# Weight-block additions of a seven-product MLP moved from VectorE to accumulating DMAs of GpSimd's queue

## The chip, the cores and the metric

The kernel runs on one core of a Trainium2 chip. The metric is the device time of one execution in microseconds. The engines are TensorE (PE: matmul; PEld: its weight load), VectorE (DVE), ScalarE (ACT), GpSimd (POOL) and SyncE (SP), which here only issues DMAs. Each engine works through its own instructions in order, and waits on semaphores for the others.

## The reference, cut to what matters

Two layers over 1024 tokens of width 1024. Each has a mixer (a gated MLP with a delta rule in layer 0, differential attention in layer 1), an MLP, and a gate at its end. The change is in the MLP:

```python
for layer in range(DEPTH):                       # 2
    ...
    hn = rms_norm(h, ln_mlp[layer])
    h = h + jnp.square(jax.nn.relu(hn @ w_mlp1[layer])) @ w_mlp2[layer]    # 1024 x 4096, 4096 x 1024
    gate = jax.nn.sigmoid(rms_norm(h, ln_ple[layer]) @ w_ple_gate[layer])
    h = h + (p[layer] @ w_ple_proj[layer]) * gate
```

## The kernel before

**Precision.** Every fp32 operand is split into hi (a rounded copy, ScalarE, line 224) and lo (operand minus hi, VectorE, line 225). A product is three matmuls, hi·hi, hi·lo and lo·hi (`mm3`, all recorded at line 78). In the profile a raw weight block is `raw` or `keep`, its hi and lo are `w`; the raw activations are `graw`, their hi and lo `g`.

**Seven products instead of eight.** Both matrix products of the MLP are taken as 2×2 blocks by the Strassen–Winograd scheme: sums and differences of weight blocks (a11, a12, a21, a22) and of activation blocks, seven products, and additions of the results. The helper `tt` (line 283) is one VectorE tensor_tensor and records nearly all those additions.

**First product (`front`, `rest`).** The 4096 hidden features go in 8 chunks `c`. `front(c)` makes two of the seven products, `rest(c)` five. A weight block is two tiles of 128×2×256 (256 KB each), loaded by `block` through SP (line 331). Before, `rest` loads a21, a22 and a11 and forms on VectorE s1 = a21 + a22 (into slot "B", of which there is one), a11 − a21 and s1 − a11; later it loads a12 and subtracts the last of these from it. The results, after relu and square, and their sums are saved to DRAM as `gd`, seven sets (`save`, line 354).

**Second product (`product2(n)`).** The seven products run in the order n = 1, 6, 5, 3, 7, 4, 2. Each has 16 steps `kt`; a step takes one weight block of 128×512 from `left(n, kt)` and one activation block of `gd`, splits both, and issues 4 × 3 matmuls of 512 columns, 192 per product. The blocks a11 (n = 1) and s1 (n = 6) stay in tiles `keep`, which lie in the space of the half's hi and lo tiles. Before, n = 6 loads a21 into `keep` and a22 into `raw`, adds them in `keep`, and subtracts a11 into `raw`; n = 5 uses `keep` as it is; n = 3 loads a12, adds a11 and subtracts s1; n = 7 loads a21 and subtracts; n = 4 and 2 only load. Results are added into `acc` and `u` after a product, on VectorE. `fetch` loads the residual `acc` in between.

**What sets the order.** A scheduler places the instructions of each engine from the program order and the pools. Pools: 8 `raw` tiles (`RB`), 12 `w` tiles (6 steps), 4 `graw` slots, 4 pairs of `g`. Every DMA of `load` (line 323) is further held behind the last matmul of the step `AHEAD` = 7 steps earlier. SP issues in order: a `graw` load that waits for its slot holds back every weight load behind it.

**At the end of a layer** `take_hs(0)` forms the row scales of the first half and broadcasts them (`rows`: 8 matmul records of `aux<-ident,r` and a copy by ScalarE, line 273).

Of the kernel before, what the change touches and what calls it, by code (L numbers as in the profile page):

```python
# [116 lines left out]
class Trunk:  # L117
# [158 lines left out]
    def mlp(self, x, x_tags, gain, w1, w2, gain_next, h_dram, p, last):  # L276
# [5 lines left out]
        def tt(out, a, b, op):  # L282
            nc.vector.tensor_tensor(out, a, b, op)  # L283
            return out
# [37 lines left out]

            self.pe.behind(nc.sync.dma_start(out, src), marks[-AHEAD])

        def block(c, r, k):

            out = []
            for i in range(2):
                out.append(self.raw(2, 256))
                r0, c0 = (4 * k + 2 * i) * P, c * 512 + r * 256  # L330
                nc.sync.dma_start(out[i], w1[r0 : r0 + 2 * P, c0 : c0 + 256].rearrange("(k p) m -> p k m", p=P))
            return out

        def product(raws, b, ps=None):

# [38 lines left out]
        def rest(c):  # L374
            u, g11 = us.pop(c), g11s.pop(c)
            g12, g21, g22 = (tiles((f"c{8 + 2 * i}", f"c{9 + 2 * i}"), "g") for i in range(3))
            v, g2 = ([self.sp.tile([P, HT], F32, tag=f"{n}{h}", name=self.nm("v"), bufs=1) for n in ("sqs", "rb")] for h in range(2))
            s1 = self.slot("B", [P, 2, 2, 256], F32, "s1")
            s1 = [s1[:, i] for i in range(2)]
            a21, a22, a11 = block(c, 1, 0), block(c, 1, 1), block(c, 0, 0)  # L380
            for i in range(2):
                tt(s1[i], a21[i], a22[i], ALU.add)
                tt(a21[i], a11[i], a21[i], ALU.subtract)
                tt(a11[i], s1[i], a11[i], ALU.subtract)
            ps = product(a21, t3)
            for i in range(2):
                nc.scalar.copy(v[i], ps[i])
            ps6 = product(a11, t2)
            if not t4:
                t4.extend(make_t4())  # L390
            for i in range(2):
                tt(u[i], u[i], ps6[i], ALU.add)
                tt(v[i], u[i], v[i], ALU.add)
            product(a22, t4, ps)
            for i in range(2):
                tt(g21[i], u[i], ps[i], ALU.add)
                relu2(g21[i], g21[i])
                tt(g11[i], g21[i], g11[i], ALU.subtract)
            save(3, c, g21)
            save(7, c, g11)  # L400
            if not t1:
                t1.extend(make_t1())
            ps = product(s1, t1)
            for i in range(2):
                tt(g22[i], v[i], ps[i], ALU.add)
                relu2(g22[i], g22[i])
            save(2, c, g22)
            a12 = block(c, 0, 1)
            for i in range(2):
                tt(a12[i], a12[i], a11[i], ALU.subtract)  # L410
            product(a12, b22, ps)
            for i in range(2):
                tt(g12[i], u[i], ps[i], ALU.add)
                relu2(g12[i], g12[i])
            save(1, c, g12)
            for i in range(2):
                tt(g2[i], g11[i], g12[i], ALU.add)
            save(6, c, g2)
            for i in range(2):
                tt(g22[i], g22[i], g2[i], ALU.subtract)  # L420
                tt(g21[i], g21[i], g2[i], ALU.subtract)
            save(4, c, g22)
            save(5, c, g21)
# [49 lines left out]
        def kept(half, k):  # L473

            return self.hp.tile([P, 1, HT], F32, tag=f"{('hi', 'lo')[k % 2]}{half}{k // 2}", name=self.nm("keep"))

        def load2(t, r, k, kt):

            r0 = (kt // 2) * 512 + k * 256 + (kt % 2) * P
            load(t, w2[r0 : r0 + P, r * 512 : (r + 1) * 512].rearrange("(k p) m -> p k m", p=P))  # L480
            return t

        def left(n, kt):
            def raw():
                return self.raw(1, HT)

            if n == 1:
                keep[0, kt] = load2(kept(1, kt), 0, 0, kt)
                return keep[0, kt]
            if n == 6:  # L490
                s1 = keep[1, kt] = load2(kept(0, kt), 1, 0, kt)
                s2 = load2(raw(), 1, 1, kt)
                tt(s1, s1, s2, ALU.add)
                return tt(s2, s1, keep[0, kt], ALU.subtract)
            if n == 5:
                return keep[1, kt]
            if n == 3:
                s4 = load2(raw(), 0, 1, kt)
                tt(s4, s4, keep[0, kt], ALU.add)
                return tt(s4, s4, keep[1, kt], ALU.subtract)  # L500
            if n == 7:
                s3 = load2(raw(), 1, 0, kt)
                return tt(s3, keep[0, kt], s3, ALU.subtract)
            return load2(raw(), int(n == 4), 1, kt)
# [42 lines left out]
            tt(acc[q][1], acc[q][1], ps[q], ALU.add)  # L547
        ps = product2(6)
        for q in range(4):
            tt(u[q], u[q], ps[q], ALU.add)  # L550
        ps = product2(5, beside={4: (0, 4), 8: (0, 0), 12: (1, 4)})
        for q in range(4):
            tt(acc[4 + q][0], acc[4 + q][0], ps[q], ALU.add)
# [12 lines left out]
        for q in range(4):  # L566
            tt(acc[4 + q][1], acc[4 + q][1], ps[q], ALU.add)
            put(4 + q, 1)
        self.take_hs(0)
        ps = product2(2)  # L570
        for q in range(4):
            tt(acc[q][1], acc[q][1], ps[q], ALU.add)
# [1604 lines left out]
```

## Time and profile before

| | us |
|---|---|
| three timed runs | 2472.01, 2472.32, 2473.27 (median 2472.32) |
| the profiled execution | 2478.68 |
| its span | 2477.0 |
| TensorE without work in the span | 18.3 |
| first product of layer 0's MLP | about 490 to 776 |
| second product of layer 0, n = 1, 6, 5, 3, 7 | from 776, 820, 865, 909 and 953 on |
| second product of layer 1, n = 1, 6, 5, 3, 7 | from 2045, 2089, 2134, 2178 and 2224 on |

Times are microseconds from the span's start. A stretch of the profile lists for each engine the busy time and in brackets the instructions, then the mean TensorE clock (1.00 is full), the share of time in which the core's 16 DMA engines were busy, and the rate they moved. In a timeline, brackets at a row's end hold the idle time before it and what ended it. In the chain of work that ended last, each piece is followed back to what released it.

### The profile page before, as it was taken

The page shows a single profiled execution, that of the slowest core. Times are in us where ns is not written, and L with a number is a line of the kernel's source. Part 1 is how long each engine was busy: PE and PEld are TensorE (multiplying, and loading weights), DVE is VectorE, ACT ScalarE, POOL GpSimd, SP SyncE. Part 2 cuts the span into 40 slices and gives each one's busy share as a digit, 9 for nine tenths or more (in the row PEclk, how much of TensorE's full clock was granted, in tenths as well). Part 3 has the DMA queues.
Part 4 walks back from the last instruction along what each step waited for, and adds up shares of the span by engine and source line. Part 5 has one row for each costly group of instructions (what it writes and reads, how often), then busy time and mean ns, then how long its engine had stood idle before and what let it go on. Part 6 is the DMA issues. An engine that isn't in the chain of part 4 may idle for free.

```text
span 2477.0 us, 39903 instructions
## 1 busy us (share of the span) xinstructions
PE 2458.7 (99%) x13501; PEld 2104.9 (85%) x13501; DVE 1857.3 (75%) x3622; ACT 1315.9 (53%) x2701; POOL 320.2 (13%) x304
## 2 busy tenths in 40 slices
PE   9999999999999999999999999999999999999999
PEld 7898998888888888888899999988878888878887
DVE  7787766697667879566568888876886677788677
ACT  6554474465455435454366666664745455435543
POOL 0231231000000000000244443341000000000010
PEclk9999999999999999999999999999999999999999
DMA  7385655467557755553347776787375558657772
GB/s 245 113 261 119 173 172 164 140 179 245 162 175 249 255 181 194 185 176 113 115 107 165 162 175 154 195 230 236 130 236 190 174 181 286 218 178 221 224 247 91
DMA packets 555029, 459.08 MB, mean 185 GB/s; under 512 B 248260, under 2 KB 416456, under 8 KB 554824
## 3 DMA queue, kind: packets, MB, share of 16 engines
q1 hardware_dynamic: 524472, 451.28, 59.8%
q10 hardware_dynamic: 29584, 3.68, 1.0%
q8 instruction: 106, 1.74, 0.3%
q0 software_dynamic: 768, 1.57, 0.2%
q14 instruction: 99, 0.81, 0.1%
HBM read 322.04 MB, written 134.37 MB: 184 GB/s over the span
## 4 chain that ended last, share of the span: by engine, by line
PE 91%; DMA 4%; DVE 3%; ACT 1%; issue 1%; SPq 0%; POOL 0%; DVEq 0%; ACTq 0%
PE mm L78 80%; PE po L78 3%; PE aux L78 2%; PE qk L78 2%; DMA raw<-in_w_mlp_dram 1%; PE tr L81 1%; DMA spill<-early 0%; DMA early<-g_dram 0%; DVE raw L283 0%; DMA aT<-a_dram 0%; DMA a_dram<-lg 0%; PE pkq L78 0%; PE pks L78 0%; PE aux L81 0%; DVE w L225 0%
## 5 line engine op out<-in xcount | busy, mean ns | idle before, releaser
L78 PE MATMUL mm<-g,w 128*128 128x512 f32 x2592 | 603.1, 394 | 2.3 <-DVE acc L283 1.8
L224 ACT CAST w<-raw 128x512 fp32r<-128x512 f32 x598 | 364.4, 617 | 446.9 <-PE mm L78 381.5
L78 PEld LDWEIGHTS mm<-g,w 128*128 128x128 f32 x2592 | 487.7, 188 | 115.5 <-ACT g L224 2.2
L78 PE MATMUL mm<-hi,w 128*128 128x512 f32 x1728 | 552.9, 397 | 0.0
L78 PE MATMUL mm<-w,hi 128*128 128x256 f32 (+2 forms) x2528 | 500.4, 294 | 0.5 <-DVE w L225 0.4
L225 DVE TENSOR_TENSOR w<-raw,w 128x512 fp32r<-128x512 f32 (+1 forms) x510 | 347.6, 690 | 163.9 <-ACT w L224 152.9
L78 PEld LDWEIGHTS mm<-w,hi 128*128 128x128 f32 x2528 | 400.2, 188 | 14.5 <-DVE w L225 0.6
L78 PEld LDWEIGHTS mm<-hi,w 128*128 128x128 f32 x1728 | 324.9, 189 | 73.7
L78 PE MATMUL mm<-w,lo 128*128 128x256 f32 (+2 forms) x1264 | 367.7, 292 | 0.0
L78 PE MATMUL mm<-lo,w 128*128 128x512 f32 x864 | 340.7, 395 | 0.0
L78 PE MATMUL mm<-t,w 128*128 128x512 f32 x1152 | 270.7, 394 | 0.9 <-ACT w L224 0.7
L78 PEld LDWEIGHTS mm<-t,w 128*128 128x128 f32 x1152 | 216.3, 188 | 52.2 <-ACT w L224 1.2
L78 PEld LDWEIGHTS mm<-w,lo 128*128 128x128 f32 x1264 | 237.8, 188 | 5.4
L78 PEld LDWEIGHTS mm<-lo,w 128*128 128x128 f32 x864 | 162.9, 188 | 36.7
L224 ACT CAST g<-graw 128x512 fp32r<-128x512 f32 x216 | 132.6, 617 | 36.7 <-PE mm L78 15.8
L225 DVE TENSOR_TENSOR g<-graw,g 128x512 fp32r<-128x512 f32 x216 | 146.9, 684 | 5.6 <-DMA gd<-g 3.8
L1067 ACT ACTIVATE lg<-lg,nm 128x128 f32<-128x128 f32 (+7 forms) x128 | 99.2, 775 | 75.0 <-DVE nm L1064 73.2
L265 POOL TENSOR_TENSOR r<-ms,mhalf 128x4 f32<-128x4 f32 x12 | 12.5, 1043 | 948.1 <-DVE ms L263 920.9
L225 POOL TENSOR_TENSOR w<-raw,w 128x512 fp32r<-128x512 f32 (+1 forms) x88 | 113.9, 1316 | 132.2 <-ACT w L224 100.5
L349 ACT ACTIVATE g<-g 128x512 f32<-128x512 f32 x96 | 60.3, 631 | 111.1 <-DVE g L283 107.2
L1064 DVE CUSTOM_DVE_ANT_0 lg<-qk,al 128x512 f32<-128x512 f32 (+3 forms) x128 | 72.3, 568 | 25.8 <-PE qk L78 22.1
L78 PE MATMUL mm<-ohi,w 128*128 128x512 f32 x256 | 86.0, 400 | 0.2 <-DVE aT L1281 0.2
(344 smaller groups left out, 3554.1 us busy)
## 6 DMA issues: line engine op xcount, KB each, us to landing
raw<-in_w_mlp_dram SPq DMA_DIRECT2D x352, 256.0 KB, 3.2
graw<-gd SPq DMA_DIRECT2D x224, 256.0 KB, 2.7
gd<-g SPq DMA_DIRECT2D x192, 256.0 KB, 3.1
raw<-in_w_ple_gate_dram SPq DMA_DIRECT2D x76, 256.0 KB, 3.5
acc<-h_dram SPq DMA_DIRECT2D x64, 256.0 KB, 4.4
keep<-in_w_mlp_dram SPq DMA_DIRECT2D x64, 256.0 KB, 4.5
raw<-in_w_in_e_dram SPq DMA_DIRECT2D x60, 256.0 KB, 3.7
h_dram<-acc SPq DMA_DIRECT2D x48, 256.0 KB, 2.3
```

Source lines behind the costliest of these rows:

```text
L78: self._next(self.engine.matmul(*a, **k))
L81: self._next(self.engine.transpose(*a, **k))
L224: self.nc.scalar.copy(hi, src)
L225: (lo_engine or self.nc.vector).tensor_tensor(lo, src, f32(hi), ALU.subtract)
L265: nc.gpsimd.tensor_tensor(r, ms, self.mhalf[:, 0:4], ALU.pow)
L349: nc.scalar.activation(g, src, AF.Relu)
L1064: nc.vector.tensor_tensor_reduce(out=lg[:, k0:k1], in0=ps[:, : k1 - k0], in1=al[:, u0 + k0 : u0 + k1], scale=-1.0, scalar=3.0e38 if c == 0 ...
L1067: nc.scalar.activation(lg[:, :n], lg[:, :n], AF.Exp, bias=nm[:, r, nch - 1 : nch], scale=-1.0, accum_out=me.sums[:, b, r : r + 1])
```

## The change

In the first product a11 is loaded before a22; the differences are a11 − a21 and from that minus a22, so the product `ps6` has the other sign and is subtracted from u. s1 is no longer added on VectorE: SP loads a21 into slot "B", and GpSimd's queue adds a22 to it in the DMA (`accum_op=ALU.add`). a12 is added in the same way onto the tile of a11, behind that tile's split, instead of an own load and a subtraction.

In the second product n = 6 loads a21 into `keep` and lets GpSimd's queue add a22; VectorE then takes a11 minus that, in place (one operation rather than two, the sign turned). n = 5 loads a21 again, into `raw`, and adds a22 by DMA. n = 3 adds a12 by DMA onto `keep`, without a load and without VectorE. n = 7, 4 and 2 are as they were. The last layer's `take_hs(0)` leaves out the broadcast of the row scales, which nothing reads there.

```diff
--- before.py
+++ after.py
@@ -322,14 +322,21 @@
 
             self.pe.behind(nc.sync.dma_start(out, src), marks[-AHEAD])
 
-        def block(c, r, k):
-
-            out = []
+        def source(c, r, k, i):
+            r0, c0 = (4 * k + 2 * i) * P, c * 512 + r * 256
+            return w1[r0 : r0 + 2 * P, c0 : c0 + 256].rearrange("(k p) m -> p k m", p=P)
+
+        def block(c, r, k, out=None):
+
+            out = out or [self.raw(2, 256) for _ in range(2)]
             for i in range(2):
-                out.append(self.raw(2, 256))
-                r0, c0 = (4 * k + 2 * i) * P, c * 512 + r * 256
-                nc.sync.dma_start(out[i], w1[r0 : r0 + 2 * P, c0 : c0 + 256].rearrange("(k p) m -> p k m", p=P))
+                nc.sync.dma_start(out[i], source(c, r, k, i))
             return out
+
+        def add_block(c, r, k, out):
+
+            for i in range(2):
+                nc.gpsimd.dma_start(out[i], source(c, r, k, i), accum_op=ALU.add)
 
         def product(raws, b, ps=None):
 
@@ -377,19 +384,21 @@
             v, g2 = ([self.sp.tile([P, HT], F32, tag=f"{n}{h}", name=self.nm("v"), bufs=1) for n in ("sqs", "rb")] for h in range(2))
             s1 = self.slot("B", [P, 2, 2, 256], F32, "s1")
             s1 = [s1[:, i] for i in range(2)]
-            a21, a22, a11 = block(c, 1, 0), block(c, 1, 1), block(c, 0, 0)
+            a21, a11, a22 = block(c, 1, 0), block(c, 0, 0), block(c, 1, 1)
             for i in range(2):
-                tt(s1[i], a21[i], a22[i], ALU.add)
                 tt(a21[i], a11[i], a21[i], ALU.subtract)
-                tt(a11[i], s1[i], a11[i], ALU.subtract)
+                tt(a11[i], a21[i], a22[i], ALU.subtract)
+            block(c, 1, 0, s1)
+            add_block(c, 1, 1, s1)
             ps = product(a21, t3)
             for i in range(2):
                 nc.scalar.copy(v[i], ps[i])
             ps6 = product(a11, t2)
+            add_block(c, 0, 1, a11)
             if not t4:
                 t4.extend(make_t4())
             for i in range(2):
-                tt(u[i], u[i], ps6[i], ALU.add)
+                tt(u[i], u[i], ps6[i], ALU.subtract)
                 tt(v[i], u[i], v[i], ALU.add)
             product(a22, t4, ps)
             for i in range(2):
@@ -405,10 +414,7 @@
                 tt(g22[i], v[i], ps[i], ALU.add)
                 relu2(g22[i], g22[i])
             save(2, c, g22)
-            a12 = block(c, 0, 1)
-            for i in range(2):
-                tt(a12[i], a12[i], a11[i], ALU.subtract)
-            product(a12, b22, ps)
+            product(a11, b22, ps)
             for i in range(2):
                 tt(g12[i], u[i], ps[i], ALU.add)
                 relu2(g12[i], g12[i])
@@ -474,10 +480,18 @@
 
             return self.hp.tile([P, 1, HT], F32, tag=f"{('hi', 'lo')[k % 2]}{half}{k // 2}", name=self.nm("keep"))
 
+        def source2(r, k, kt):
+            r0 = (kt // 2) * 512 + k * 256 + (kt % 2) * P
+            return w2[r0 : r0 + P, r * 512 : (r + 1) * 512].rearrange("(k p) m -> p k m", p=P)
+
         def load2(t, r, k, kt):
 
-            r0 = (kt // 2) * 512 + k * 256 + (kt % 2) * P
-            load(t, w2[r0 : r0 + P, r * 512 : (r + 1) * 512].rearrange("(k p) m -> p k m", p=P))
+            load(t, source2(r, k, kt))
+            return t
+
+        def add2(t, r, k, kt):
+
+            self.pe.behind(nc.gpsimd.dma_start(t, source2(r, k, kt), accum_op=ALU.add), marks[-AHEAD])
             return t
 
         def left(n, kt):
@@ -488,16 +502,12 @@
                 keep[0, kt] = load2(kept(1, kt), 0, 0, kt)
                 return keep[0, kt]
             if n == 6:
-                s1 = keep[1, kt] = load2(kept(0, kt), 1, 0, kt)
-                s2 = load2(raw(), 1, 1, kt)
-                tt(s1, s1, s2, ALU.add)
-                return tt(s2, s1, keep[0, kt], ALU.subtract)
+                s2 = keep[1, kt] = add2(load2(kept(0, kt), 1, 0, kt), 1, 1, kt)
+                return tt(s2, keep[0, kt], s2, ALU.subtract)
             if n == 5:
-                return keep[1, kt]
+                return add2(load2(raw(), 1, 0, kt), 1, 1, kt)
             if n == 3:
-                s4 = load2(raw(), 0, 1, kt)
-                tt(s4, s4, keep[0, kt], ALU.add)
-                return tt(s4, s4, keep[1, kt], ALU.subtract)
+                return add2(keep[1, kt], 0, 1, kt)
             if n == 7:
                 s3 = load2(raw(), 1, 0, kt)
                 return tt(s3, keep[0, kt], s3, ALU.subtract)
@@ -547,7 +557,7 @@
             tt(acc[q][1], acc[q][1], ps[q], ALU.add)
         ps = product2(6)
         for q in range(4):
-            tt(u[q], u[q], ps[q], ALU.add)
+            tt(u[q], u[q], ps[q], ALU.subtract)
         ps = product2(5, beside={4: (0, 4), 8: (0, 0), 12: (1, 4)})
         for q in range(4):
             tt(acc[4 + q][0], acc[4 + q][0], ps[q], ALU.add)
@@ -566,7 +576,7 @@
         for q in range(4):
             tt(acc[4 + q][1], acc[4 + q][1], ps[q], ALU.add)
             put(4 + q, 1)
-        self.take_hs(0)
+        self.take_hs(0, rows=not last)
         ps = product2(2)
         for q in range(4):
             tt(acc[q][1], acc[q][1], ps[q], ALU.add)
```

By count: VectorE makes 160 tensor_tensor operations fewer, GpSimd's queue issues 160 accumulating DMAs of 256 KB, and the second product moves 144 weight blocks per layer instead of 112.

How it moves the instructions, in layer 0. First VectorE in the middle of n = 6; before, step 12 is the tile keep_1731, its second block raw_1732, its w numbers 1733 and 1734, and the g of steps 9 and 10 are g_1716 and g_1723:

```order
L283 TENSOR_TENSOR keep_1731_9332<-keep_1731_9332,raw_1732_9334 128x512
L225 TENSOR_TENSOR w_1720_9283<-raw_1718_9278,w_1719_9282 128x512
L283 TENSOR_TENSOR raw_1725_9306<-keep_1724_9304,keep_1613_8864 128x512
L283 TENSOR_TENSOR raw_1732_9334<-keep_1731_9332,keep_1619_8888 128x512
L225 TENSOR_TENSOR g_1716_9261<-graw_1714_9258,g_1715_9260 128x512
L283 TENSOR_TENSOR keep_1738_9360<-keep_1738_9360,raw_1739_9362 128x512
L225 TENSOR_TENSOR w_1727_9311<-raw_1725_9306,w_1726_9310 128x512
L283 TENSOR_TENSOR raw_1739_9362<-keep_1738_9360,keep_1625_8912 128x512
L225 TENSOR_TENSOR w_1734_9339<-raw_1732_9334,w_1733_9338 128x512
L225 TENSOR_TENSOR g_1723_9289<-graw_1721_9286,g_1722_9288 128x512
```

After, steps 11 to 13 are keep_1697, keep_1703 and keep_1709, and the g of steps 8 to 10 are g_1684, g_1690 and g_1696:

```order
L283 TENSOR_TENSOR keep_1697_9266<-keep_1597_8848,keep_1697_9266 128x512
L225 TENSOR_TENSOR w_1693_9245<-keep_1691_9240,w_1692_9244 128x512
L225 TENSOR_TENSOR g_1684_9199<-graw_1682_9196,g_1683_9198 128x512
L225 TENSOR_TENSOR w_1699_9271<-keep_1697_9266,w_1698_9270 128x512
L225 TENSOR_TENSOR g_1690_9225<-graw_1688_9222,g_1689_9224 128x512
L283 TENSOR_TENSOR keep_1703_9292<-keep_1603_8872,keep_1703_9292 128x512
L283 TENSOR_TENSOR keep_1709_9318<-keep_1609_8896,keep_1709_9318 128x512
L225 TENSOR_TENSOR w_1705_9297<-keep_1703_9292,w_1704_9296 128x512
L225 TENSOR_TENSOR g_1696_9251<-graw_1694_9248,g_1695_9250 128x512
```

Of the two operations on each block, the sum into `keep` is gone; the subtraction now stands on `keep` itself, with the subtractions of steps 12 and 13 ahead of the g of step 10.

Then SP in the same place, before (graw_1721 is step 10's, graw_1728 step 11's):

```order
L323 DMA raw_1725_9306<-in_w_mlp2_dram 128x512
L323 DMA graw_1721_9286<-gd_966_5752 128x512
L323 DMA keep_1731_9332<-in_w_mlp2_dram 128x512
L323 DMA raw_1732_9334<-in_w_mlp2_dram 128x512
L323 DMA graw_1728_9314<-gd_966_5752 128x512
L323 DMA keep_1738_9360<-in_w_mlp2_dram 128x512
L323 DMA raw_1739_9362<-in_w_mlp2_dram 128x512
```

And after (graw_1694 is step 10's, keep_1703 step 12's):

```order
L323 DMA graw_1688_9222<-gd_965_5751 128x512
L323 DMA keep_1697_9266<-in_w_mlp2_dram 128x512
L323 DMA graw_1694_9248<-gd_966_5752 128x512
L323 DMA keep_1703_9292<-in_w_mlp2_dram 128x512
L323 DMA graw_1700_9274<-gd_966_5752 128x512
L323 DMA keep_1709_9318<-in_w_mlp2_dram 128x512
```

One weight load of two per step is gone from SP; a step's weight load stands behind the activation load of two steps before. The second block now goes through GpSimd's queue, where the accumulates of the steps follow each other.

Last VectorE at the start of n = 3, where the results of n = 5 are added up, before (raw_1879 to raw_1903 are a12 blocks, acc and u results):

```order
L225 TENSOR_TENSOR w_1875_9967<-raw_1873_9962,w_1874_9966 128x512
L225 TENSOR_TENSOR g_1866_9921<-graw_1864_9918,g_1865_9920 128x512
L283 TENSOR_TENSOR acc_1533_8582<-acc_1533_8582,u_1540_8589 128x512
L283 TENSOR_TENSOR acc_1533_8582<-acc_1533_8582,u_1541_8590 128x512
L283 TENSOR_TENSOR acc_1533_8582<-acc_1533_8582,u_1542_8591 128x512
L283 TENSOR_TENSOR raw_1885_10014<-raw_1885_10014,keep_1589_8764 128x512
L283 TENSOR_TENSOR raw_1891_10040<-raw_1891_10040,keep_1595_8792 128x512
L993 MEMSET ql_2524_12565 128x512
L283 TENSOR_TENSOR raw_1897_10066<-raw_1897_10066,keep_1601_8816 128x512
L283 TENSOR_TENSOR raw_1885_10014<-raw_1885_10014,keep_1696_9192 128x512
L283 TENSOR_TENSOR raw_1891_10040<-raw_1891_10040,keep_1703_9220 128x512
L225 TENSOR_TENSOR w_1881_9993<-raw_1879_9988,w_1880_9992 128x512
```

And after, a few steps into n = 3:

```order
L225 TENSOR_TENSOR w_1868_10018<-keep_1679_9188,w_1867_10017 128x512
L225 TENSOR_TENSOR w_1873_10041<-keep_1685_9214,w_1872_10040 128x512
L225 TENSOR_TENSOR g_1866_10001<-graw_1864_9998,g_1865_10000 128x512
L225 TENSOR_TENSOR w_1878_10064<-keep_1691_9240,w_1877_10063 128x512
L225 TENSOR_TENSOR g_1871_10024<-graw_1869_10021,g_1870_10023 128x512
L225 TENSOR_TENSOR w_1883_10087<-keep_1697_9266,w_1882_10086 128x512
L225 TENSOR_TENSOR g_1876_10047<-graw_1874_10044,g_1875_10046 128x512
L225 TENSOR_TENSOR w_1888_10110<-keep_1703_9292,w_1887_10109 128x512
```

The two additions on every a12 block are gone; a step has one w and one g split.

## The prediction

> **What bounds the kernel now.** First the page: the busy row, then the chain of work that ended last.
>
> ```profile
> span 2477.0 us, 39903 instructions
> PE 2458.7 (99%) x13501; PEld 2104.9 (85%) x13501; DVE 1857.3 (75%) x3622; ACT 1315.9 (53%) x2701; POOL 320.2 (13%) x304
> PE 91%; DMA 4%; DVE 3%; ACT 1%; issue 1%; SPq 0%; POOL 0%; DVEq 0%; ACTq 0%
> ```
>
> TensorE is busy for 2458.7 of 2477.0 us. Whatever the change does on VectorE, it can win only what TensorE idles (18.3 us over the whole kernel) or loses to a lower clock. So the second view is busy time by stretch, one stretch per MLP stage, to see how much of that lies where additions are removed. The rows are the second half of layer 0's first MLP product (633 to 776), its MLP2 products 1, 6, 5, 3 (776 to 953), the opening of layer 1's first MLP product, and layer 1's product 3.
>
> ```profile
> core 0: us, PE busy (x) PEld busy (x) DVE busy (x) ACT busy (x) POOL busy (x), PEclk, DMA share, GB/s
> 633.00:776.00 143.00, 143.00 (x619) 116.06 (x618) 98.12 (x156) 73.35 (x129) 0.00 (x0) 1.00 0.55 184
> 776.00:820.00 44.00, 44.00 (x192) 35.73 (x191) 30.57 (x50) 23.16 (x42) 0.00 (x0) 1.00 0.86 291
> 820.00:865.00 45.00, 45.00 (x197) 36.55 (x196) 38.77 (x65) 21.32 (x38) 0.00 (x0) 1.00 0.77 248
> 865.00:909.00 44.00, 44.00 (x192) 35.81 (x191) 31.71 (x51) 17.92 (x32) 0.00 (x0) 1.00 0.60 190
> 909.00:953.00 44.00, 43.43 (x188) 34.73 (x187) 42.34 (x70) 18.41 (x32) 3.03 (x2) 1.00 0.58 190
> 1756.00:1812.00 56.00, 54.56 (x241) 43.44 (x240) 51.07 (x85) 36.69 (x66) 1.01 (x1) 1.00 0.40 118
> 2178.00:2224.00 46.00, 44.22 (x185) 35.49 (x184) 40.42 (x68) 17.76 (x32) 0.00 (x0) 0.96 0.55 174
> ```
>
> The reader is to see that the MLPs already run without a gap except at three places: product 3 of layer 0 (0.57 us idle), product 3 of layer 1 (1.78 us idle, and a mean clock of 0.96 over 46 us, another 1.84 us), and the opening in layer 1 (1.44 us). VectorE's 38.8 busy of 45 us in product 6 cost TensorE nothing. The largest gap is explained by the chain that ended last in layer 1's product 3, and by the queue's timeline a little earlier.
>
> ```profile
> 2172.61 0.42 SPq L323 DMA_DIRECT2D raw<-in_w_mlp_dram  x1
> ...
> 2175.53 0.69 DVE L283 TENSOR_TENSOR raw<-raw,keep 128x512 f32<-128x512 f32 x1 [0.55 <-DMA raw<-in_w_mlp_dram]
> ...
> 2177.34 0.68 DVE L225 TENSOR_TENSOR g<-graw,g 128x512 fp32r<-128x512 f32 x1
> ...
> 2178.05 0.32 SPq L323 DMA_DIRECT2D graw<-gd  x1
> ...
> 2178.42 0.43 SPq L323 DMA_DIRECT2D raw<-in_w_mlp_dram  x1
> ```
>
> ```profile
> 2178.42 2.89 DMA raw<-in_w_mlp_dram
> ...
> 2183.23 0.61 DVE g L225
> ...
> 2184.22 4.79 DMA raw<-in_w_mlp_dram
> ...
> 2190.25 0.69 DVE acc L283
> 2190.94 0.14 issue
> 2191.08 9.15 PE mm L78 x32
> ```
>
> This is a closed loop: a weight block lands, VectorE's addition takes it, a g split further back in the same in-order engine follows, that frees a graw slot, SP issues the graw load and only then the next weight load. One turn is 2178.42 − 2172.61 = 5.81 us for two steps; four products in 953 − 776 = 177 us make a step 2.77 us, so TensorE needs 5.54 for two. The loop loses a little per turn, and when one load takes 4.79 us instead of 2.89 the lead is gone: TensorE stands, then runs at a lower clock.
>
> **The change part by part.** What leaves VectorE, by form of instruction:
>
> ```profile
> L283 DVE TENSOR_TENSOR raw<-raw,raw 128x512 f32<-128x512 f32 x64 | 43.7, 686 | 27.6 <-DMA raw<-in_w_mlp_dram 27.4
> L283 DVE TENSOR_TENSOR raw<-raw,keep 128x512 f32<-128x512 f32 x64 | 43.1, 691 | 8.4 <-DMA raw<-in_w_mlp_dram 8.1
> L283 DVE TENSOR_TENSOR keep<-keep,raw 128x512 f32<-128x512 f32 x32 | 22.0, 688 | 12.1 <-DMA raw<-in_w_mlp_dram 12.0
> L283 DVE TENSOR_TENSOR s<-raw,raw 128x512 f32<-128x512 f32 x32 | 21.5, 688 | 8.6 <-DMA raw<-in_w_mlp_dram 8.5
> ```
>
> All 64 raw<-raw,keep (product 3), all 32 keep<-keep,raw (product 6), all 32 s<-raw,raw, and 32 of the 64 raw<-raw,raw (the a12 part) go: 64 × 0.691 + 64 × 0.688 + 32 × 0.686 = 110.2 us of VectorE. Nearly all of it lies beside a TensorE without a gap and is worth nothing in itself. What it is worth:
>
> *Product 3.* Per step, two of four VectorE operations and SP's weight load go; the accumulate needs no earlier load and waits behind no graw. The loop above no longer exists: 0.57 + 1.78 + 1.84 = **4.2 us**. Next late there would be the g path alone, two operations (1.4 us) per 2.77 us step.
>
> *Opening of layer 1.* There VectorE is the chain:
>
> ```profile
> 1800.32 1.20 DVE u L283 x2
> 1801.52 0.60 DVE w L225
> 1802.12 0.67 DVE s L283 x2
> ...
> 1808.07 1.28 DVE g L283 x2
> ...
> 1811.61 3.50 PE mm L78 x14
> ```
>
> The s pair (two times 0.6) leaves it, so **1.2** of the 1.44 us. In layer 0's opening nothing idles.
>
> *Last layer's unused row broadcast:*
>
> ```profile
> 2333.66 1.06 PE L78 MATMUL aux<-ident,r 128*128 128x128 f32 x8
> ...
> 2334.47 1.86 PE L78 MATMUL mm<-g,w 128*128 128x512 f32 x7
> ```
>
> The next matmul starts 0.81 us after the first of the eight: **0.8 us**. Signs and the order of subtractions cost nothing: as many operations of the same form.
>
> The ceiling is 4.2 + 1.2 + 0.8 = **6.2 us**, 0.25%.
>
> What is added: 32 accumulates per layer in the first product, 48 in the second, and in product 5 a reload of 16 blocks that were kept before. In the first product 16 MB of loads stay as many; DMA is busy 0.55 and POOL 0.00 there, so I cost it at nothing; that cover is the whole front of the next chunk between the request of s1 and its use. If it is gone, product s1 of a chunk waits. The first s1 of each layer is requested before the stage ahead has ended, and its accumulate waits in POOL's order for its load. Behind it stand, in layer 0, the last chunk's factor fo and its product with z; in layer 1 three lo splits of the output weights and the last block's of. POOL's rows there:
>
> ```profile
> 417.89 1.01 POOL L1915 TENSOR_TENSOR fo<-so,mhalf 128x4 f32<-128x4 f32 x1 [13.69 <-DVE so L1913]
> ...
> 1716.09 1.37 POOL L1128 TENSOR_TENSOR of<-osq,mhalf 128x4 f32<-128x4 f32 x1 [25.15 <-DVE osq L1126]
> ```
>
> POOL idles 13.7 and 25.2 us ahead of these, so a load of 3 to 4 us fits in: nothing; without that cover, up to 4 us per layer.
>
> *Product 6, the one added wait.* VectorE's subtraction now waits for load, then accumulate. Behind it in VectorE's order stands an older g split, which frees graw, behind which SP holds the next load. In the new order (its rows stand with the change) a turn advances three or four steps, 3.5 × 2.77 = 9.7 us. The turn costs 0.3 (graw issue) + load + accumulate + 2 to 3 VectorE operations at 0.6 (1.5). The loads of product 6, and the nearest rows for a DMA of POOL's queue against SP's:
>
> ```profile
> graw<-gd SPq DMA_DIRECT2D x17, 256.0 KB, 2.9
> keep<-in_w_mlp_dram SPq DMA_DIRECT2D x12, 256.0 KB, 4.0
> ```
>
> ```profile
> by_token<-t SPq DMA_DIRECT2D x48, 64.0 KB, 2.6
> by_token<-t POOLq DMA_DIRECT2D x16, 64.0 KB, 4.5
> ```
>
> Load: 2.9 to 4.0. Accumulate: no row shows one. Lower bound 2.9 (as an SP load), upper bound 9 (twice 4.5, if the second operand is read in a second pass). I take 4.5, the nearest row, since it has the queue. The turn is then 0.3 + 2.9 + 4.5 + 1.5 = 9.2, or 10.3 with the slower load: even with the 9.7 that TensorE needs. Over five turns of a product the slower one loses 3 us, inside the two to three steps by which operands run ahead (5.5 to 8 us: there are four g pairs, one of them in use). So I take 0. At 9 us it would be (0.3 + 4 + 9 + 1.5 − 9.7) × 5 = 25, less a lead of 7: 18 us per layer, the upper end. In product 5 nothing of VectorE waits between load and split, and loads run further ahead; the same prices, so also 0.
>
> The Trainium skill bears on this price: "DMA: Bandwidth & Descriptors", section "Anatomy of one DMA — SWDGE (gpsimd) path", fits 2.0 us plus bytes / 436e3 for one DMA of that path, so 2.6 us for 256 KB, and the turn would be 7.3. The trace speaks against it: 4.5 us for 64 KB, where the fit gives 2.15.
>
> *DMA engines.* Product 1 moves 291 GB/s at a share of 0.86, so 338 at full share: 0.775 us of all engines per 256 KB. With loads seven steps ahead, product 6's stretch holds 9 × 3 of its own, 7 × 3 of product 5's and 4 acc blocks: 52 × 0.775 = 40.3 of 45 us (0.90). Product 5's holds 9 × 3 + 8 + 7 × 2 = 49, 38 of 44 (0.86). Product 1 carries 0.86 without a gap, so at plain cost these are hidden; I take 0.5 us in all.
>
> **Sum.** −6.2 + 0.5 = −5.7 against the profiled execution (2478.68 us, span 2477.0). That one ran 6.4 us over the median 2472.32, and the late load of 4.79 us may be part of that; the timed runs may hold less of the 3.6 us of layer 1's product 3. I take off 0.4 for it: **−5.3, 2467.0**.
>
> **Rivals.**
> 1. *DMA waits take VectorE's place, about even.* An accumulate of 6 us makes the turn 10.7 to 11.8 in product 6: five turns lose 5 to 10, less a lead of 7, so up to 3 us per layer; −5.3 + 6 = about 2473. Likewise if the timed runs lack product 3's stall altogether: 2472.3 − 2.6 = 2470. For it: the load's own 4.0. Against: product 1's loads at 0.86 share come without a gap. 2470 to 2476.
> 2. *The accumulate costs the engines twice* (it reads its destination too). Then 16 × 0.775 = 12.4 us more in each of the two stretches: 52.7 of 45 and 50.4 of 44. Excess 7.7 + 6.4 = 14 us per layer at worst; the share at which the 0.86 rises to 1 absorbs nothing more, but product 3 with 0.58 takes the late part of the second. From 1 + 4.7/12.4 = 1.4 times on, product 6 is bound by DMA. So +10 to +28, less 5.3: 2477 to 2495, at its middle 2485. It is the slower rival. For it: 338 GB/s is the most that a stretch here shows, and no row shows an accumulate. Against: VectorE gives up a load's buffer, so requests may run further ahead.
>  The Trainium skill has such a rule: "Collectives: The Full Stack", section "The bandwidth ceiling: the fold count and why AG ≠ RS ≠ AR", says that a DMA add needs two source reads and so halved a reduce's rate against a copy's. No run here shows it yet.
> 3. *The change doesn't do what it says*: POOL's issues are delayed by its own work. POOL is busy 0.00 in every MLP2 stretch but product 3 (3.03 us), so hardly: worth under 1 us.
>
> **How the numbers follow.** Forecast (2465 to 2470) 0.43; about even (2470 to 2476) 0.25; engines doubled or late accumulates (2477 to 2495) 0.29; below 2465 0.03. About 0.2%, 4.9 us, is what a measurement of this kernel tells from no change, so the marks are 2467.4 and 2477.3. Of the forecast's 0.43 some 0.33 lies below 2467.4: faster 0.36, same 0.34, slower 0.30. The range 2464 to 2488 leaves out the upper part of the second rival (0.11) and little below.
>
> **What would show it.** Right: product 3's stretches show 44 of 44 us at clock 1.00 in both layers; VectorE near 24 us busy in product 3 (42.3 less 26 operations) and near 30 in product 6 (38.8 less 13); no aux matmuls at the end. Accumulates landing in 4 to 5 us carry the forecast, 6 us the first rival, a DMA share near 1.0 in products 6 and 5 with TensorE waiting for w or keep the second. It is wrong if TensorE idles in products 1 to 5 of layer 0, where it now does not, or if the first MLP product waits for s1.

## The result and the profile after

The changed kernel takes 2526.2 us (median of 4 runs, 2520.5 to 2530.1) against 2472.8 us (4 runs): a ratio of 1.0214, 95% interval 1.0201 to 1.0226, so 53 us slower. The prediction said 2467.0, with a range of 2464 to 2488.

The page of the changed kernel, busy times and the chain that ended last:

```profile
span 2528.4 us, 40102 instructions
PE 2473.5 (98%) x13493; PEld 2106.8 (83%) x13493; DVE 1761.8 (70%) x3462; ACT 1312.4 (52%) x2700; POOL 478.4 (19%) x464
PE 86%; DMA 8%; DVE 2%; issue 1%; ACT 1%; SPq 0%; POOL 0%; DVEq 0%; POOLq 0%; ACTq 0%
```

VectorE lost 95 us of work (1857.3 to 1761.8) and TensorE's idle time still rose from 18.3 to 54.9 us; DMA went from 4% to 8% of the chain. TensorE's busy time rose too, by 14.8 us, with 8 instructions fewer: in part because its clock was lower after stalls, as the stretches below show.

Where: each product of the second MLP matrix has 192 matmul records in the profile, so the start of each can be counted out. Durations in us, from one product's first matmul to the next one's:

| | layer 0: n = 6 | 5 | 3 | 7 | layer 1: n = 6 | 5 | 3 | 7 |
|---|---|---|---|---|---|---|---|---|
| before | 44.4 | 44.5 | 45.3 | 44.4 | 44.3 | 46.4 | 46.0 | 44.4 |
| after | 64.0 | 53.7 | 44.6 | 44.5 | 64.0 | 55.2 | 44.5 | 44.6 |

By this count the stage times given ahead of the prediction are 11 us early: n = 6 starts at 831.0 in layer 0 and 2100.4 in layer 1, because the first four steps of n = 1 carry another name (`mm<-hi,w`) and had been left out. The late load in layer 1 that the prediction dwells on thus lies at the end of product 5, not in product 3. The kernel before in layer 1, products 5 and 3 by the counted starts: the idle time is in the first row, the lower clock in the second.

```profile
2145.00:2191.00 46.00, 44.30 (x192) 35.65 (x190) 34.53 (x57) 19.10 (x34) 0.00 (x0) 1.00 0.58 178
2191.00:2237.00 46.00, 45.92 (x192) 37.30 (x193) 41.12 (x68) 17.79 (x32) 0.00 (x0) 0.96 0.59 188
```

Products 6 and 5 lose 19.6 + 9.2 and 19.7 + 8.8 = 57.3 us; product 3 gains 0.7 and 1.5. The stretches of the changed kernel, by those starts (columns as in the prediction: n = 6 and 5 of layer 0, the same of layer 1, then the opening of layer 1's first product):

```profile
831.00:895.00 64.00, 50.79 (x192) 38.61 (x190) 30.30 (x49) 20.00 (x36) 12.28 (x15) 0.92 0.87 209
895.00:949.00 54.00, 48.34 (x195) 35.94 (x196) 31.86 (x51) 21.28 (x38) 16.33 (x19) 1.00 1.02 265
2125.00:2189.00 64.00, 49.71 (x193) 37.65 (x191) 30.15 (x49) 20.08 (x36) 12.12 (x15) 0.95 0.85 210
2189.00:2244.00 55.00, 49.63 (x193) 37.86 (x193) 31.23 (x50) 21.07 (x37) 21.81 (x26) 0.94 1.02 257
1746.00:1802.00 56.00, 55.46 (x260) 45.48 (x259) 47.04 (x77) 33.86 (x61) 2.02 (x2) 1.00 0.51 170
```

The kernel before, products 6 and 5 of layer 0:

```profile
831.00:875.00 44.00, 44.00 (x192) 35.79 (x191) 35.54 (x58) 19.15 (x34) 0.00 (x0) 1.00 0.73 232
875.00:920.00 45.00, 44.99 (x196) 36.29 (x195) 35.55 (x58) 18.57 (x33) 0.00 (x0) 1.00 0.56 181
```

Two different pictures. In product 5 the DMA engines are full (1.02). In product 6 they are not (0.87 on average), and still TensorE idles 13.2 of 64 us and is busy 50.8 us for 192 matmuls that took 44.0 before. Of these 6.8 us the clock explains 44.0 / 0.92 − 44.0 = 3.8, about a fifth of the whole loss; the rest is not clock, for product 5 of layer 0 has the same at clock 1.00 (48.3 us for 195 matmuls, which would take 44.7). What TensorE waited for most, over the whole kernel (us in total, times, longest):

```profile
PE mm L78 <- DVE g L225: 23.0, 18, 4.3
PE mm L78 <- ACT g L224: 12.0, 10, 3.0
```

The kernel before has 0.6 us of the first, and the second is not in its list, which goes down to 0.2 us:

```profile
PE mm L78 <- DVE g L225: 0.6, 1, 0.6
```

TensorE waits for g, not for the accumulated weight block. The chain of work in product 6 of the changed kernel (start, duration, what) shows why; one turn, from the issue of one activation load to the next:

```profile
852.66 0.32 SPq L323
...
853.04 4.19 DMA keep<-in_w_mlp_dram
...
857.27 0.48 issue
...
857.76 5.90 DMA keep<-in_w_mlp_dram
...
864.30 0.69 DVE w L225
...
866.19 0.61 DVE g L225
866.82 0.32 SPq L323
```

SP issues the load of a21 behind a graw; 4.19 us later it lands, GpSimd issues the accumulate, which lands after 5.90 us; only then VectorE can subtract, and the g split queued behind that subtraction, with three other splits between them, frees the next graw. This turn takes 866.82 − 852.66 = 14.2 us; the next, with an accumulate of 7.44 us, takes 15.8. At 64.0 / 16 = 4.0 us a step, 14.2 us are 3.5 steps, for which TensorE needs 9.7.

The DMA queues in product 5 of the changed kernel (packets, MB, share of 16 engines; then issues with the median time to landing) show the other half:

```profile
q0 software_dynamic: 2731, 4.98, 52.5%
q1 hardware_dynamic: 5087, 9.26, 49.7%
...
graw<-gd SPq DMA_DIRECT2D x19, 256.0 KB, 6.0
raw<-in_w_mlp_dram POOLq DMA_DIRECT2D x12, 256.0 KB, 7.0
raw<-in_w_mlp_dram SPq DMA_DIRECT2D x10, 256.0 KB, 8.1
acc<-h_dram SPq DMA_DIRECT2D x8, 256.0 KB, 8.1
keep<-in_w_mlp_dram POOLq DMA_DIRECT2D x7, 256.0 KB, 12.0
```

q0, GpSimd's queue, takes 52.5% of the engines for 4.98 MB: 0.525 × 54 × 16 / 2731 = 0.166 us a packet. SP's q1 takes 49.7% for 9.26 MB: 0.497 × 54 × 16 / 5087 = 0.084. For 256 KB that is 1.49 us of all engines for an accumulate, 0.76 for a load.

### The profile page after: what moved, and what is told of

Same layout as the page of the kernel before. It is cut to its first block, busy times and chain, and to the rows that moved or that the text cites. A ratio compares the mean times of both kernels' runs of the same rounds, so it can differ in the third digit from the quotient of the medians.

```text
span 2528.4 us, 40102 instructions
## 1 busy us (share of the span) xinstructions
PE 2473.5 (98%) x13493; PEld 2106.8 (83%) x13493; DVE 1761.8 (70%) x3462; ACT 1312.4 (52%) x2700; POOL 478.4 (19%) x464
## 3 DMA queue, kind: packets, MB, share of 16 engines
q0 software_dynamic: 32000, 43.53, 10.3%
## 4 chain that ended last, share of the span: by engine, by line
PE 86%; DMA 8%; DVE 2%; issue 1%; ACT 1%; SPq 0%; POOL 0%; DVEq 0%; POOLq 0%; ACTq 0%
PE mm L78 75%; DMA keep<-in_w_mlp_dram 4%; PE po L78 3%; DMA raw<-in_w_mlp_dram 3%; PE qk L78 2%; PE aux L78 2%; PE tr L81 1%; DVE w L225 1%; DVE g L225 1%; PE pkq L78 0%; PE pks L78 0%; ACT w L224 0%; SPq L323 0%; PE pst L78 0%; DMA raw<-in_w_out_e_dram 0%
## 5 line engine op out<-in xcount | busy, mean ns | idle before, releaser
L78 PE MATMUL mm<-g,w 128*128 128x512 f32 x2592 | 622.5, 400 | 38.5 <-DVE g L225 23.0
L224 ACT CAST w<-raw 128x512 fp32r<-128x512 f32 (+1 forms) x566 | 345.8, 616 | 408.9 <-PE mm L78 295.9
L225 DVE TENSOR_TENSOR w<-raw,w 128x512 fp32r<-128x512 f32 (+1 forms) x478 | 328.4, 692 | 242.9 <-ACT w L224 234.1
L224 ACT CAST w<-keep 128x512 fp32r<-128x512 f32 x96 | 59.1, 619 | 142.1 <-DVE keep L283 81.5
L494 POOL DMA_DIRECT2D keep<-in_w_mlp_dram x64 | 58.4, 1228 | 218.2 <-DMA keep<-in_w_mlp_dram 191.9
```

The costliest lines, as they stand in the source:

```text
L78: self._next(self.engine.matmul(*a, **k))
L224: self.nc.scalar.copy(hi, src)
L225: (lo_engine or self.nc.vector).tensor_tensor(lo, src, f32(hi), ALU.subtract)
L494: self.pe.behind(nc.gpsimd.dma_start(t, source2(r, k, kt), accum_op=ALU.add), marks[-AHEAD])
```

## The experiments

Two theories after the result. **Turn**: the serial wait in product 6 (load, accumulate, VectorE's in-order subtraction, graw) is longer than TensorE's pace. **Engines**: an accumulate takes twice the DMA time and the engines are full. Each run's figures stand beside the kernel before, run on the same chip.

**The first product and the row broadcast alone.** The second product (`left` and the sign of u) is as before; of the change there remains:

```diff
 a21, a11, a22 = block(c, 1, 0), block(c, 0, 0), block(c, 1, 1)
...
 add_block(c, 1, 1, s1)
...
 add_block(c, 0, 1, a11)
...
 self.take_hs(0, rows=not last)
```

> The change in the first MLP product (s1 and a12 by accumulating DMAs) and the row broadcast of the last layer left out; the second product as before. The changed kernel shows no idle TensorE in the first product, so both theories of the loss (a longer turn in product 6, and DMA engines that are full in product 5) expect no loss here: 2.8 us of TensorE's loss go (about 0.8 for the broadcast, up to 1.2 at the opening of layer 1), 2470 to 2473 us, products 6, 5, 3 as before (44.4, 44.5, 45.3 and 44.3, 46.4, 46.0 us). If accumulates in the first product cost something that the stages hide, more than 2476 us.

Measured: 2472.9 us against 2474.0, ratio 0.9994 (0.9985 to 1.0003). The 64 accumulates of the first product cost nothing, and what they and the broadcast save is within the measurement. In the profile, the opening of layer 1's first product idles 0.54 us instead of 1.44, in this run and in the changed kernel. Layer 1's products 5 and 3 take 44.6 us each here, with their code as before: the stall of 46.4 and 46.0 us was not in this execution.

**The second product's accumulates as plain writes.** The sums are left out; transfers, queue and order stay.

```diff
-nc.gpsimd.dma_start(t, source2(r, k, kt), accum_op=ALU.add)
+nc.gpsimd.dma_start(t, source2(r, k, kt))
```

> The changed kernel, but in the second product GpSimd's DMAs write their block instead of adding it (the additions are left out there, the transfers, their queue, their order and all waits stay). Engines theory: a packet of that queue falls from 0.166 us to about 0.084, product 5 goes from 54 to 44.5 us and product 6 to about 45, 2472 to 2478 us in all. Turn theory: product 5 recovers too, but product 6 keeps a turn of 0.3 + 4 + 0.5 + 4.5 (a plain DMA of that queue) + 1.5 = 10.8 us for 3.5 steps, 3.1 us a step, so 49 to 52 us instead of 64, and 2483 to 2492 us in all.

Measured: 2485.8 us against 2474.0, ratio 1.0043 (1.0027 to 1.0058). Products 6 and 5 take 53.6 and 45.7 us in layer 0, 52.8 and 49.3 in layer 1; the profiled execution took 2493.1 us, 7 more than the median, so the median run lost less than these figures. The stretches of this run for the two products of layer 0:

```profile
828.00:881.00 53.00, 47.37 (x190) 37.50 (x190) 29.65 (x48) 19.07 (x34) 7.53 (x14) 0.94 0.71 237
881.00:927.00 46.00, 45.39 (x195) 36.10 (x194) 30.39 (x50) 20.16 (x36) 10.17 (x19) 1.00 0.93 318
```

GpSimd's queue in product 5 of this run:

```profile
q0 software_dynamic: 1539, 5.02, 31.3%
```

The same bytes over the same queue: product 5 moves 318 GB/s instead of 265 and nearly recovers in layer 0 (in layer 1 it gets back 5.9 of its 8.8 us), so most of its loss was the price of the add. A plain write costs 0.313 × 46 × 16 / 1539 = 0.150 us a packet, and as its packets are larger, 0.75 us of all engines per 256 KB, like a load of SP: the double price is the add's, not the queue's. Product 6, with a DMA share of only 0.71, keeps 9 of its 20 us in this profile: that is the turn.

**Accumulates in product 6 alone.**

```diff
-                s1 = keep[1, kt] = load2(kept(0, kt), 1, 0, kt)
-                s2 = load2(raw(), 1, 1, kt)
-                tt(s1, s1, s2, ALU.add)
-                return tt(s2, s1, keep[0, kt], ALU.subtract)
+                s1 = keep[1, kt] = add2(load2(kept(0, kt), 1, 0, kt), 1, 1, kt)
+                return tt(raw(), keep[0, kt], s1, ALU.subtract)
```

> The first product, product 5 and product 3 as before; only product 6 adds a22 by DMA, and the subtraction goes to a raw tile so that product 5 can use the kept sum. DMA work in product 6's stretch: 9 steps of 4 units of 0.675 us, 7 graw loads ahead and 4 acc blocks, 47 units or 32 us of 44. Engines theory: that fits, product 6 stays at 44 to 46 us, 2470 to 2477 us. Turn theory: the wait for load, accumulate and subtraction is all still there, product 6 takes 58 to 64 us in both layers, product 5 about 44.5, 2500 to 2513 us.

Measured: 2501.6 us against 2474.0, ratio 1.0109 (1.0095 to 1.0123); product 6 takes 58.4 and 58.3 us, product 5 45.1 and 45.8. Product 6 of layer 0:

```profile
829.00:887.00 58.00, 48.23 (x192) 37.63 (x191) 33.77 (x55) 22.44 (x40) 8.56 (x10) 0.94 0.79 195
```

No transfers are added in this kernel, and VectorE has one operation a step less; half of the change's loss is there all the same. The engines were busy for 0.79 of that stretch, so on average they were not full; this is what the turn theory forecast (58 to 64 us). The 5.6 us that are missing to 64.0 probably came with product 5's extra transfers, ten of which are issued in product 6 of the changed kernel; no run tested that by itself.

**The same with a plain write in place of the add.** (The sum is left out.)

```diff
-nc.gpsimd.dma_start(t, source2(r, k, kt), accum_op=ALU.add)
+nc.gpsimd.dma_start(t, source2(r, k, kt))
```

> As the run with accumulates in product 6 alone, but GpSimd's DMA writes a22 over a21 instead of adding it (the addition is left out in product 6; transfers, queue, order and waits stay). If the serial wait is what costs (load, then a second DMA, then VectorE's in-order subtraction) and the price of an add only lengthens it: a turn of 0.3 + 3.6 + 0.5 + 4.5 + 1.5 = 10.4 us for 3.5 steps, product 6 46 to 50 us, 2477 to 2485 us in all. If only the doubled engine time costs: 44.5 us and 2472 to 2476 us. If the waits alone cost all of it: 55 us or more, over 2494 us.

Measured: 2484.7 us against 2473.6, ratio 1.0044 (1.0029 to 1.0058); in its profile product 6 takes 47.5 and 49.1 us. GpSimd's queue and its DMAs in product 6 of layer 0, in the run with adds (first, a stretch of 58 us) and in this one (47 us):

```profile
q0 software_dynamic: 1750, 3.17, 33.5%
keep<-in_w_mlp_dram POOLq DMA_DIRECT2D x10, 256.0 KB, 4.8
```

```profile
q0 software_dynamic: 821, 2.67, 17.4%
keep<-in_w_mlp_dram POOLq DMA_DIRECT2D x10, 256.0 KB, 2.9
```

Worked out as above, 256 KB cost 1.61 us of all engines with the add and 0.80 without. By these profiles, of the 14 us of product 6 alone some 3 to 5 are the serial second DMA as such, and 9 to 11 that it adds; but the profiled execution was the shortest of its four (2480.2 us), and by the medians (28 us lost with adds, 11 without, over two layers) it is 5.5 and 8.3. The theories are not rivals: an add doubles the engine time and lands later (4.8 us instead of 2.9), and that lengthens the turn.

**Loads of product 6 four steps earlier,** first in the changed kernel, then with accumulates in product 6 alone.

```diff
+                if n == 6:
+                    for j in range(kt, min(NK, kt + 5)):
+                        if (1, j) not in keep:
+                            keep[1, j] = add2(load2(kept(0, j), 1, 0, j), 1, 1, j)
                 a = self.parts(left(n, kt), nc.vector)
```

> The changed kernel, with the load and accumulate of product 6 requested four steps earlier in the program, so that SP issues a weight load ahead of the graw loads of four more steps and a turn advances 5.5 to 6 steps (15 to 16 us) instead of 3.5. All transfers stay. Turn theory: product 6 falls from 64 to 45 to 50 us; product 5 stays full of DMA (50 to 56 us), 2490 to 2505 us. Engines theory alone: the sum of products 6 and 5 stays near 118 us, 2520 to 2530 us.

> As the run with accumulates in product 6 alone, with their loads requested four steps earlier in the program. If the long turn is what cost 14 us per layer there, it goes: DMA work of 0.79 x 58 = 46 us, of which some 6 fit into product 1, so product 6 takes 44.5 to 48 us, 2473 to 2481 us in all. If the accumulates cost it in another way, product 6 stays above 52 us, over 2490 us.

Measured: 2502.9 us against 2474.0 (ratio 1.0118, 1.0104 to 1.0131) with products 6 and 5 at 51.8 and 55.7 us in layer 0 (50.6 and 55.7 in layer 1); and 2487.9 against 2474.0 (ratio 1.0057, 1.0043 to 1.0071) with product 6 at 52.5 and 51.3. Moving requests without changing a transfer takes 12 to 13 us from product 6 of the changed kernel, as the turn theory said; product 5, still full, gains nothing. The second run missed its forecast of 44.5 to 48: the earlier requests win back 6 or 7 of its 14 us. Its stretches of products 1 and 6 in layer 0:

```profile
782.00:826.00 44.00, 44.00 (x192) 35.58 (x190) 24.63 (x39) 19.96 (x36) 7.04 (x8) 1.00 0.98 297
826.00:878.00 52.00, 46.52 (x192) 36.57 (x191) 33.28 (x53) 20.56 (x36) 6.85 (x8) 0.97 0.75 197
```

The earlier requests filled product 1 (0.98 instead of 0.88), and half the accumulates landed there, after 9.5 us by the median: the start of product 6 still came late. What the rest of the loss there consists of was not tested.

**Accumulates in product 5 alone.**

```diff
             if n == 5:
-                return keep[1, kt]
+                return add2(load2(raw(), 1, 0, kt), 1, 1, kt)
```

> The kernel before, but product 5 loads a21 again and adds a22 by DMA instead of using the kept sum; everything else as before. No VectorE subtraction waits for the accumulate here. Engines theory: product 6's stretch gets 7 blocks of two transfers in advance (7 x 3 units of 0.675, 14 us) on 0.73 x 44 = 32 us, so 46 of 44; product 5's gets 9 x 3 units on 0.56 x 45 = 25, so 43 of 44: DMA is about full, products 6 and 5 take 89 to 95 us together instead of 89 to 91, 2474 to 2484 us in all. Turn theory: as SP's weight load stands in the same place as elsewhere and the accumulate only delays the split, nothing is lost, 2472 to 2475 us.

Measured: 2504.8 us against 2474.0, ratio 1.0125 (1.0111 to 1.0139), beyond both forecasts: product 5 takes 57.9 and 60.0 us, product 3 46.3 and 47.1. The chain of that run in product 5 of layer 0:

```profile
895.35 9.66 DMA acc<-h_dram
...
906.93 0.61 DVE acc L283
907.54 0.81 POOL raw L488
...
910.16 8.95 DMA raw<-in_w_mlp_dram
```

With the engines near full (0.92 of 58 us) the fetch of a residual block landed after 9.7 us, VectorE's in-order addition of it waited, then an accumulate of 9.0 us. The expectation had counted engine time only, not whom the late transfers hold up. That reading is from the chain; no run tested it on this kernel.

**Accumulates in product 3 alone,** with a11's part of the sum formed in place in product 5.

```diff
                 a = self.parts(left(n, kt), nc.vector)
+                if n == 5:
+                    tt(keep[1, kt], keep[0, kt], keep[1, kt], ALU.subtract)
...
             if n == 3:
-                s4 = load2(raw(), 0, 1, kt)
-                tt(s4, s4, keep[0, kt], ALU.add)
-                return tt(s4, s4, keep[1, kt], ALU.subtract)
+                return add2(keep[1, kt], 0, 1, kt)
```

> The kernel before, but a11 minus the kept sum is formed in place in product 5 (behind its split), and product 3 only adds a12 to that by DMA, so VectorE has 2, 1 and 0 block additions a step in products 6, 5 and 3 instead of 2, 0 and 2, and product 3 has no weight load of SP. No added transfers. The prediction's term for product 3 says 0.6 us in layer 0 and up to 3.6 in layer 1 go: products 5 and 3 take 44.4 to 44.6 us each in both layers, 2469 to 2473 us. If accumulates of 8 to 10 us to landing hold product 3 up, more than 2478 us.

Measured: 2473.6 us against 2474.0, ratio 1.0002 (0.9993 to 1.0011), no gain where 1 to 5 us were expected. Product 3 takes 44.4 us in both layers, so its accumulates are hidden and its stall is gone; layer 1's product 5 takes 48.6 in the profile, whose execution took 2475.8.

**That together with the first product and the broadcast.** (Both edits above.)

> The run before this one (only product 3 adds by DMA) together with the first product's accumulates and the row broadcast left out in the last layer. The three parts that showed no loss: 1 us from the latter two (as measured alone) and what product 3 gives: 2468 to 2472 us, ratio 0.998 to 0.9995.

Measured: 2473.0 us against 2474.0, ratio 0.9994 (0.9985 to 1.0003), where 2468 to 2472 us were expected. In the profiled execution, which at 2476.6 us was the longest of eleven, layer 1's product 5 takes 49.3 us, products 6, 3 and 7 and all of layer 0's 44.5 to 44.6. The chain there:

```profile
2158.50 9.04 DMA acc<-h_dram
...
2167.56 0.04 DVE acc L283
...
2169.51 22.68 PE mm L78 x90
```

Again a fetched residual block that lands late, and VectorE's in-order addition. With the stall of product 3 gone, this wait came next in that execution.

**Early fetches:** with the run above, on the kernel before alone, and on a version without any accumulating DMA (a11's part formed in place in product 5 as above, but in product 3 a12 is loaded to a raw tile and `keep` is added there by one VectorE operation; no row broadcast in the last layer).

```diff
-        def fetch(h, m):
-            for k in range(m, m + 4):
+        def fetch(h, m, n=4):
+            for k in range(m, m + n):
...
-        ps = product2(6)
+        ps = product2(6, beside={**{8 + i: (0, 4 + i, 1) for i in range(4)}, **{12 + i: (0, i, 1) for i in range(4)}})
...
-        ps = product2(5, beside={4: (0, 4), 8: (0, 0), 12: (1, 4)})
+        ps = product2(5, beside={i: (1, 4 + i, 1) for i in range(4)})
```

> The run with accumulates in product 3, the first product and no row broadcast, with the 12 fetches of acc blocks taken out of product 5 in fours and requested one per step from product 6's step 8 on. In that run layer 1's product 5 still took 49.3 us: VectorE's in-order addition of u waited for a fetch that landed after 9.0 us. If that is the last loss, product 5 takes 44.5 us in both layers and the time falls by 3 to 5 us to 2467 to 2470 us; if the fetches now crowd product 6, it stays at 2472 or rises.

> The kernel before, with nothing changed but the same earlier, single fetches. Layer 1's product 5 falls from 46.4 to 44.5 us, product 3 with its four VectorE operations a step stays at 45.3 in layer 0: 2470 to 2473 us, ratio 0.9985 to 1.0.

> No accumulating DMA at all: the kernel before, with the subtraction of a11 formed in place in product 5, so that VectorE has 2, 1 and 1 block additions a step in products 6, 5 and 3, the early fetches and no row broadcast in the last layer. If what helps is the even spread of VectorE's work and not the DMA adds, it is within 2 us of the run with accumulates in product 3: 2467 to 2471 us.

Measured, in this order, against 2473.6 us: 2469.5 (ratio 0.9987, 0.9978 to 0.9996), 2474.6 (1.0001, 0.9992 to 1.0010) and 2471.3 (0.9992, 0.9983 to 1.0001). The first is the only version whose interval lies below the kernel before. Its stretches of products 6, 5 and 3, both layers:

```profile
827.00:872.00 45.00, 45.00 (x196) 36.49 (x195) 39.03 (x63) 19.58 (x35) 3.44 (x4) 1.00 0.92 294
872.00:916.00 44.00, 44.00 (x192) 35.70 (x191) 34.13 (x57) 18.14 (x32) 2.54 (x3) 1.00 0.47 117
916.00:961.00 45.00, 45.00 (x196) 36.48 (x195) 30.08 (x50) 18.38 (x32) 9.92 (x11) 1.00 0.75 190
2095.00:2139.00 44.00, 44.00 (x191) 35.69 (x190) 38.81 (x64) 18.74 (x33) 3.43 (x4) 1.00 0.93 300
2139.00:2184.00 45.00, 45.00 (x196) 36.46 (x195) 35.08 (x57) 18.56 (x33) 10.19 (x12) 1.00 0.74 169
2184.00:2228.00 44.00, 44.00 (x192) 35.67 (x191) 28.61 (x47) 18.06 (x33) 0.00 (x0) 1.00 0.46 144
```

TensorE shows no idle time in them. Against the version without accumulating DMAs its gain of 1.8 us lies inside the intervals, and inside the 2 us that were set beforehand as the sign that the even spread of VectorE's work helps and not the adds. So it isn't shown that accumulating DMAs, in product 3 or in the first product, have a part in these 4 us; the fetches alone, on the kernel before, gave nothing (layer 1's product 5 still took 45.9 us).

## Why the prediction was wrong

*What bounds the kernel.* Right: 95 us of VectorE's work were worth nothing in themselves. The stage boundaries were 11 us off, which blurred product 3 and product 5 but not the sums over them; VectorE in layer 0's product 3 fell by 12 us to 30.2, not by 18 to 24.

*The terms that go.* Right in kind. Product 3 no longer stalls (44.6 and 44.5 us), the opening of layer 1 idles 0.5 instead of 1.4 us, the eight broadcast matmuls are gone. The size was too large for the timed runs: all of these together, without products 6 and 5, gave 1.1 us, not 6.2. Two things stand in the profiles: a late residual fetch took the stall's place in layer 1's product 5 (49.3 us), and the stall itself is not in every execution (the run with only the first product changed has 44.6 and 44.6 us there). The sum took 3.6 us for it from one execution that ran 6.4 us over the median, and allowed 0.4 for that. What share each has in the timed runs is open.

*Product 6, the one added wait.* This is the step that failed: "So I take 0." The turn was the right mechanism, with 10.3 us at most by the chosen value. It measured 14.2: 0.4 for SP, the load 4.2 (said: 2.9 to 4.0), the accumulate 5.9 instead of 4.5, 0.5 between the load's landing and GpSimd's issue that was not counted, and 3.2 on VectorE, five operations, instead of 1.5. The nearest row, a DMA of 64 KB in small pieces on the same queue, told nothing of an add. The stated upper end (18 us per layer) was close to the 19.6 measured, but by luck: it had 9 us for the accumulate and too little for VectorE, and its discount of 7 us for a lead did not hold, for TensorE idled 1.0 and 2.2 us within the first 6 us of product 6. Nor did that end reach the forecast: 18 us in each of two layers would have meant about 2503 us, and the range ended at 2488.

*Product 5, "so also 0".* Wrong by 9 us per layer, for the reason that the second rival gave: 49 transfers, 16 of them at double price, come to 50.4 us of all engines where the stretch had 44; it took 53.7, at a share of 1.02. The accumulate's 1.49 us per 256 KB against the load's 0.76 is 1.96 times; the rival had asked for 2. The rule of the Trainium skill that was weighed there ("Collectives: The Full Stack", section "The bandwidth ceiling: the fold count and why AG ≠ RS ≠ AR": an add needs two source reads) agrees with this trace in its price: 0.166 against 0.084 us a packet. The other rule ("DMA: Bandwidth & Descriptors", section "Anatomy of one DMA — SWDGE (gpsimd) path", 2.6 us for 256 KB) the prediction had set aside for the 4.5 us row; a plain write of 256 KB on that queue landed after 2.9 us, near the rule, while an add took 4.8 in the same place.

*How the cases were combined.* The rivals were priced each by itself, late accumulates up to 6 us and full engines up to 28. They came together: the doubled time made each accumulate later, that lengthened the turn, and product 5's added transfers probably put another 5.6 us per layer into product 6. The lower clock of product 6, 0.92 in layer 0, was in no case. Hence 53 us where the upper rival ended at 22 above the kernel before.

*The rest.* The first s1 of each layer, requested ahead of its stage, and GpSimd's order cost nothing that the timed run of the first product shows, as said. Of the signs given, TensorE idle in layer 0's products came true, and an accumulate landing after 5.9 us and more; TensorE did not wait for w or keep, as the second rival had it, but for g.

## What to carry to other kernels

An accumulating DMA is not a load that adds for free: price it at two transfers of engine time, and put it where its landing time of 5 to 12 us stands on no loop. It cost nothing, and gained nothing that is shown, where its sum is needed late: in product 3, with the target ready long before and seven steps of lead, and in the first product. It lost where a load, the add and an in-order engine's next operation follow each other inside one pipeline turn (product 6), and where added transfers fill the engines (product 5). Before relieving an engine at 75%, ask which wait in its stage ends last; when a stall of two microseconds is removed, look for the next late transfer, here the residual fetch.

## What the runs showed of the hardware that was not expected

The accumulate's packets of 2 KB cost 0.166 us of an engine's time against 0.084 for a load's; issuing one of 256 KB kept GpSimd itself busy for 0.84 us, as in the turn shown above at 857.76. Plain writes on GpSimd's queue went in larger packets: 821 for 2.67 MB in product 6 of the run with plain writes, against 1750 for 3.17 MB with adds. And TensorE's clock, 1.00 in the MLP stretches before but for the one right behind a stall (0.96), fell to 0.92 and 0.95 over the 64 us of product 6, with stalls of 1 to 5 us. In layer 0 it was 0.50 for three times 3.4 us (from 838.0, 865.3 and 882.4 on) and 1.00 between. Not every stall brings that: product 5 of layer 0 ended with one of 2.3 us, and the clock stayed at 1.00.
